# Queries and keys of stick-breaking heads as 2x2 block products behind the value projection, kept in DRAM

## The chip, the cores and the metric

One core of a Trainium2 chip runs the kernel. The metric is the device time in microseconds of one execution; the kernel before takes 1210.2 us (median of 3 runs, 1209.5 to 1210.64). TensorE (PE) multiplies matrices, VectorE (DVE), ScalarE (ACT) and GpSimd (POOL) work on elements, and SyncE (SP) issues nearly all transfers between DRAM and on-chip memory. Every engine works through its own queue in order; a wait at its head holds up all that stands behind it.

## The reference

One layer over 1024 frames of width 1024, in float32:

```python
h = rmsnorm(x, norm1_g)
proj = h @ w_in                      # 1024 x 3072
qa, ka, va, qb, kb, vb = split(proj) # 512 columns each: 8 heads of 64
ya = chunked_attention(qa, ka, va, rel_bias)      # group A: softmax over a band of 9 chunks
yb = stick_breaking_attention(qb, kb, vb)         # group B: causal, a cumulative product in place of softmax
x = x + concat(rmsnorm(ya, norm_a_g), rmsnorm(yb, norm_b_g)) @ w_out
x = x + conv_gated_mlp(rmsnorm(x, norm2_g), ...)  # up-projection, width-3 conv, silu gate, down-projection
return rmsnorm(x, final_g)
```

The change concerns the 1024 x 512 queries qb and the 1024 x 512 keys kb of group B.

## The kernel before, in words

Numbers are float32. Each operand of a large product is split into a high part (rounded to the format that TensorE takes) and a low part (the remainder), and a product is three matmuls: high x high, high x low, low x high (`mm3`, L144). `split` (L127) makes the two parts: a copy on ScalarE, then a subtraction, mostly on VectorE.

**Values first.** `all_v` (L241) makes the values of both groups as a product in 2 x 2 blocks with seven block products in place of eight (the Strassen-Winograd scheme). The normed input, without its row scale rn1, is h; split by features (k below or above 512) and frames (lo, hi), it gives the blocks b11, b21, b12, b22, of which b11, b21 and b22 are used as they are (tiles hh, hl), and four sums and differences t1 to t4, each of four tiles of 512 columns. The right-hand tiles of t1 and t3 share t_high[0] and t_low, one after the other; those of t2 and t4 share t_high[1]; t4's low parts lie where t3's were. Steps are pairs (p, k), product p and piece k, in the order p = 1, 2, 5, 6, 7, 3, 4. `extra(n)` (L385) hangs other work on a step: squares of x's rows for rn1, and at the last steps the results scaled by rn1 (`give`, L375), which go to DRAM (v_d). The four results c11 go first, then m5 and u2 (eight), and after the last step c21 (four).

**Pair 0 of group B.** Heads come in pairs n (0 to 3 are group B, 4 to 7 group A). Right behind v, L1105 to L1117 project query and key of pair 0 plainly: for each of two halves of the frames, 8 pieces of k with three matmuls, 48 matmuls for the query and 48 for the key; L1113 and L1115 in between spread rn1 over the columns (8 transposes). Each half is scaled, split and laid in the tiles qa, qb, ka, kb, la, lb that the scores want (`stack_q`, `stack_k`): a head's high and low rows on the two halves of the partitions.

**Attention with filler.** Group B (L1207 on) goes through 4 pairs x 8 query blocks x 2 heads = 64 items in the order ORDER_B; per item TensorE makes scores (zb), ScalarE a sigmoid, VectorE a scan (acts), and two items later TensorE transposes (tpb) and then multiplies with v (yb). Group A (L1266 on) goes through 4 pairs x 8 blocks with a softmax. Between these, TensorE gets filler: a generator (`filler`, L1126) gives the projections of pairs 1 to 7 in pieces of three matmuls, and then the group-B half of the output projection (pb). How much filler follows each item is set by RATE_B, LEAD_B, RATES_A and LEAD_A; `ready` (L1147) draws more when a planner (`Flow`, L485), which keeps a reckoned time for each engine, holds that the next step would wait. What filler is left after group A covers the norms there. For pairs 1 to 7 the second arrangement of the rows is made by on-chip transfers (`move`, L662).

The order on VectorE, ScalarE, GpSimd, SP and TensorE is that in which the code is written or the planner issues it; no scheduler reorders it. SP's transfers use eight semaphores in turn, so a transfer is issued only when the eighth one before it has landed.

Behind attention stand the rest of the output projection (pa), the up-projection (`up_pair`, L1772, which already uses seven products for the 2 x 2 blocks of each pair of column tiles), the convolution, and the down-projection, also in blocks.

Of the kernel before, what the change touches and what calls it, by code (L numbers as in the profile page):

```python
# [16 lines left out]
P = 128  # L17
T = 1024
# [18 lines left out]
RATE_B, LEAD_B = 19.0, 8.0  # L37
RATES_A, LEAD_A = (18.0, 22.0, 23.0, 20.0), 6.5
# [24 lines left out]
def tile_hybrid_block(  # L63
# [128 lines left out]
    with tc.tile_pool(name="kp", bufs=2) as kp:  # L192
# [42 lines left out]
        hh, hl, pre = [], [], []  # L235
# [5 lines left out]
        def all_v():  # L241
# [29 lines left out]
            ]  # L271
            row = area(kp.tile([P, D], F32, tag="rb", name="row", bufs=1))
# [47 lines left out]
            def factors(p, k):  # L320
# [14 lines left out]
                    4: (t_high[1][k], t_low[k], b[:, lo]),  # L335
# [3 lines left out]
            def parts(p, k):  # L339
                if p in (1, 2):  # L340
# [15 lines left out]
            raw0 = []  # L356
# [28 lines left out]
            def extra(n):  # L385
# [6 lines left out]
                if steps[n] == (7, 2):  # L392
                    for j in range(4):
                        S.copy(m5[j], X[j])
                    raw0.append(wp.tile([P, D], F32, tag="wr", name="raw0_0", bufs=1))
                    nc.sync.dma_start(raw0[0], w_in[12])
                if steps[n] == (3, 0):
                    for j in range(4):
                        plus(m5[j], m5[j], Y[j], V)
                if steps[n] == (3, 3):  # L400
# [3 lines left out]
                    raw0.append(kp.tile([P, D], F32, tag="rb", name="raw0_1", bufs=1))  # L404
                    nc.sync.dma_start(raw0[1], w_in[16])
# [6 lines left out]
                if steps[n] == (4, 2):  # L412
                    pre.append(weights(None, "qk01", raw=raw0[1]))
                if steps[n] == (4, 3):
                    give(staged("c21"), 1, 0, Y)

# [37 lines left out]
            for n, (p, k) in enumerate(steps):  # L454
# [16 lines left out]
                extra(n)  # L471

        S.preload_act_table_set("sqrt_and_others")
        all_v()
# [102 lines left out]

        class Banks:
# [19 lines left out]
        for n in range(1, 8):  # L598
            ct = 12 + n if n < 4 else n - 4
# [62 lines left out]
        def move(t, x, y, a, b):  # L662

            return load(128, lambda: nc.sync.dma_start(r32(x[b, t]), r32(y[a, t])))

        def stack_q(n, outs):
            s = 6 * (n % 2)
            qa, qb = slot(s, f"qa{n}", F32R), slot(s + 1, f"qb{n}", F32R)
            qk_of[n] = [qa, qb]

            def half(g):

                t, r = {}, rows(g)
                project = on_v(GW, lambda: scaled(outs[g], g, 0.125, f"q{n}", t))

                def low_rows(x, a, b):
                    return load(128, lambda: nc.sync.dma_start(r32(x[b, r]), t["f"][a, :]))

                if n == 0:
                    return fs.chain(  # L680
                        project,
                        on_s(GW, lambda: S.copy(qa[A, r], t["f"][A, :])),
                        on_s(GW, lambda: S.copy(qb[B, r], t["f"][B, :])),
                        on_v(GW, lambda: sub(qa[B, r], t["f"][A, :], qa[A, r]), "VL"),
                        on_v(GW, lambda: sub(qb[A, r], t["f"][B, :], qb[B, r]), "VL"),
                    )
                return fs.chain(
                    project,
                    on_s(GW, lambda: S.copy(qa[:, r], t["f"])),
                    on_v(GW, lambda: sub(t["f"].bitcast(F32R), t["f"], qa[:, r]), "VL"),  # L690
                    move(r, qb, qa, B, A),
                    low_rows(qb, B, B),
                    low_rows(qa, A, B),
                )

            for g in range(G):
                yield half(g)

        def stack_k(n, outs):
            s = 6 * (n % 2)  # L700
# [1480 lines left out]
```

## Time and profile before

| what | us |
| --- | --- |
| median of 3 runs | 1210.2 |
| profiled execution, span from first to last instruction | 1208.5 |
| TensorE busy | 1196.2 |
| VectorE busy | 922.2 |
| ScalarE busy | 676.1 |
| v in blocks ends, q of pair 0 begins | 85.98 |
| first scores of group B | 116.88 |
| up-projection in steady state | 606 to 980 |

In lists of instructions the columns are start, duration, engine, line, operation, output<-input, shapes and count; in a group's row the busy time, the mean in ns, then the idle time of the engine before it and what ended that. In rows of windows come the stretch, its length, the busy time of each engine with its count of instructions, the clock that TensorE was granted (1.00 is full), the busy share of the 16 DMA engines, and GB/s. TensorE's instructions overlap, so durations in a list add to more than the time passed; in the chain each has only its share.

### The profile page before, as it was taken

To read this page: it belongs to the slowest core of one execution; us is meant where nothing else is said; L and a number is where in the kernel's file an instruction comes from. 1 tells how busy PE (TensorE), PEld (TensorE's weight loads), DVE (VectorE), ACT (ScalarE), POOL (GpSimd) and SP (SyncE) were. 2 spreads that over 40 slices of the span, in tenths; PEclk is the share of its full clock that TensorE was granted. 3 is DMA by queue.
4 is the path that set the end of the run, shared out by engine and by line. 5 is a ranking of instruction groups with operands and counts; after the bars stand their busy time and mean duration, and the time that the engine had idled before them with its cause. 6 is when DMAs were issued, how large, how long until landed. Compare 5 with 4: busy or idle time off the path is not lost.

```text
span 1208.5 us, 17319 instructions
## 1 busy us (share of the span) xinstructions
PE 1196.2 (99%) x6476; PEld 997.9 (83%) x6476; DVE 922.2 (76%) x1405; ACT 676.1 (56%) x1196; POOL 178.9 (15%) x188
## 2 busy tenths in 40 slices
PE   9999999999999999999999999999999999999997
PEld 6788888888888888888878888888888888888887
DVE  7955776967676678568997877778677779969896
ACT  7864564656676657334665555555555455444424
POOL 0003211122213121232000000000000023132036
PEclk9999999999999999999999999999999999999998
DMA  8254343443534472143133222231222296420003
GB/s 300 92 186 141 85 134 79 133 113 100 162 84 101 128 227 82 37 147 114 36 105 105 71 87 88 70 105 70 87 88 71 71 374 252 182 97 1 1 1 140
DMA packets 64529, 137.30 MB, mean 114 GB/s; under 512 B 6839, under 2 KB 22327, under 8 KB 64446
## 3 DMA queue, kind: packets, MB, share of 16 engines
q1 hardware_dynamic: 64302, 136.10, 34.5%
q8 instruction: 51, 0.84, 0.3%
q14 instruction: 32, 0.26, 0.1%
q10 hardware_dynamic: 144, 0.11, 0.0%
HBM read 91.34 MB, written 28.33 MB: 99 GB/s over the span
## 4 chain that ended last, share of the span: by engine, by line
PE 93%; DVE 4%; ACT 2%; issue 1%; POOL 0%; DVEq 0%; ACTq 0%; POOLq 0%
PE u_c L1596 9%; PE u_e L1596 9%; PE u_a L1596 9%; PE dz L2095 8%; PE q_p L147 7%; PE k_p L147 7%; PE u_b L1596 5%; PE dj L2095 4%; PE dm L2095 4%; PE pb L147 3%; PE pa L147 3%; PE v_x L459 3%; PE tpb L874 3%; PE yb L888 3%; PE u L1648 3%; PE v_y L459 2%
## 5 line engine op out<-in xcount | busy, mean ns | idle before, releaser
L847 DVE TENSOR_TENSOR_SCAN acts<-zb,first 128x128 f32<-128x128 f32 (+7 forms) x64 | 86.6, 1353 | 39.6 <-ACT zb L856 39.3
L856 ACT ACTIVATE zb<-zb 128x128 f32<-128x128 f32 (+7 forms) x64 | 40.8, 637 | 55.0 <-PE zb L839 54.6
L125 POOL TENSOR_TENSOR dx_0wl<-dr,dx_0wh 128x512 fp32r<-128x512 f32 x1 | 1.4, 1366 | 412.6 <-ACT dx_0wh L1862 412.6
L1620 DVE SCALAR_TENSOR_TENSOR vt<-cv,cst,vt 128x1023 f32<-128x1023 f32 (+1 forms) x44 | 58.2, 1322 | 2.2 <-ACT vt L1614 1.4
L1620 DVE SCALAR_TENSOR_TENSOR gt<-cg,cst,gt 128x1023 f32<-128x1023 f32 (+1 forms) x44 | 56.4, 1281 | 1.4 <-ACT gt L1614 0.6
L969 ACT ACTIVATE pa<-sa,sta 128x640 f32<-128x640 f32 (+4 forms) x64 | 42.7, 668 | 23.1 <-DVE sta L955 21.2
L125 POOL TENSOR_TENSOR q_l<-q_r,q_h 128x256 fp32r<-128x256 f32 x28 | 22.2, 823 | 188.7 <-ACT q_h L629 188.7
L1614 ACT ACTIVATE gt<-cg,cst 128x1024 f32<-128x1024 f32 x22 | 27.4, 1246 | 37.0 <-DVE cg L1488 37.0
L147 PE MATMUL k_p<-hTh,k_h 128*128 128x512 f32 x112 | 47.7, 426 | 0.0
L147 PE MATMUL q_p<-hTh,q_h 128*128 128x512 f32 x112 | 46.5, 416 | 0.0
L878 ACT COPY tb<-tpb 128x128 f32<-128x128 f32 (+3 forms) x96 | 43.1, 485 | 5.8 <-PE tpb L874 4.7
L994 ACT COPY pta<-tpa 128x512 f32<-128x512 f32 (+3 forms) x80 | 36.1, 479 | 14.3 <-PE tpa L990 14.2
L147 PE MATMUL k_p<-hTh,k_l 128*128 128x512 f32 x112 | 43.9, 392 | 0.0
L147 PE MATMUL k_p<-hTl,k_h 128*128 128x512 f32 x112 | 43.9, 392 | 0.0
L147 PE MATMUL q_p<-hTh,q_l 128*128 128x512 f32 x112 | 43.8, 391 | 0.0
L147 PE MATMUL q_p<-hTl,q_h 128*128 128x512 f32 x112 | 43.8, 391 | 0.0
L955 DVE TENSOR_REDUCE sta<-sa 128x1 f32<-128x640 f32 (+4 forms) x64 | 42.0, 657 | 1.6
L874 PE MATMUL tpb<-ident,acts 128*128 128x128 f32 x288 | 42.9, 276 | 0.0
L1485 DVE TENSOR_TENSOR up_r<-up_r 128x512 f32<-128x512 f32 x60 | 41.3, 688 | 0.8
L990 PE MATMUL tpa<-ident,pa 128*128 128x128 f32 x240 | 39.0, 278 | 1.0 <-ACT pta L994 0.4
L874 PEld LDWEIGHTS tpb<-ident,acts 128*128 128x128 f32 x288 | 33.3, 141 | 5.4 <-issue 2.6
L990 PEld LDWEIGHTS tpa<-ident,pa 128*128 128x128 f32 x240 | 27.6, 140 | 9.5 <-issue 4.7
(1315 smaller groups left out, 3930.8 us busy)
## 6 DMA issues: line engine op xcount, KB each, us to landing
up_r<-in_w_up_dram SPq DMA_DIRECT2D x44, 512.0 KB, 3.5
act<-vt SPq DMA_DIRECT2D x22, 512.0 KB, 2.6
dr<-in_w_dn_dram SPq DMA_DIRECT2D x20, 512.0 KB, 6.3
dr<-act SPq DMA_DIRECT2D x20, 512.0 KB, 8.1
wv<-in_w_v_dram SPq DMA_DIRECT2D x16, 256.0 KB, 5.4
xin<-in_xT_dram SPq DMA_DIRECT2D x16, 256.0 KB, 5.4
row<-in_x_rows_dram SPq DMA_DIRECT2D x16, 256.0 KB, 2.6
v<-v_d SPq DMA_DIRECT2D x8, 512.0 KB, 5.9
```

What stands on the lines that cost most here:

```text
L147: PE.matmul(o, w[:, sl], t[:, rows(g)], start=first and i == 0, stop=last and i == 2,)
L459: PE.matmul(bank[j], t[:, cols(j)], w, start=p in (1, 5) and k == 0 and i == 0, stop=k == 3 and i == 2, skip_group_check=True,)
L847: V.tensor_tensor_scan(out=a[:, :w], data0=z, data1=first[:, :w], initial=1.0, op0=ALU.mult, op1=ALU.max,)
L874: PE.transpose(tp[:, cols(b)], self.a[h][:, cols(b0 + b)], ident)
L878: mine.append(flow.add(on_s(m * P, lambda o=o, tp=tp: S.copy(o, tp))))
L955: V.tensor_reduce(out=st[:, 0:1], in_=full, axis=AX.XY if nk == 5 else AX.X, op=ALU.max, negate=True,)
L969: on_s(w + 170, lambda: S.activation(po, full, AF.Exp, bias=st[:, 0:1], accum_out=st[:, 1:2])),
L990: PE.transpose(tp[:, cols(b)], self.pr[src][:, cols(c)], ident)
L1485: eng.tensor_tensor(out=out, in0=a, in1=b, op=ALU.subtract)
L1596: PE.matmul(o, w[:, cols(k)], t, start=start and k == 0 and i == 0, stop=k == 3 and i == 2, skip_group_check=True,)
L1620: V.scalar_tensor_tensor(out=t[:, : T - lag], in0=o[:, lag:], scalar=c1(c + ct), in1=t[:, : T - lag], op0=ALU.mult, op1=ALU.add,)
L2095: PE.matmul(o[m], w[:, cols(m)], t, start=i in (0, 1, 4, 5) and p == ps_[0] and j == 0, stop=p == ps_[-1] and j == 2, skip_group_check=True,)
```

## The change

Queries and keys of all four pairs of group B are made right behind v, by seven block products each pair; v's sums t1 to t4 are used again as right-hand blocks. The left-hand blocks come from the weights: q's two column halves (k below and above 512) are a11 and a12, k's second half a22, and s1 to s4 are sums of the halves.

- t1 and t2 are overwritten in v, so `keep` stores them to DRAM (16 transfers of 256 KB, in steps 9, 11, 12 and 14), and `bring_back` loads them again at step (4, 0) (8 transfers of 512 KB). t3 stays; t4 gets low tiles of its own (t4_low).
- `bring_raw` loads raw weights; `Pieces` makes sums and splits of a pair's weights. At steps (4, 0) to (4, 3) pair 0's first pieces are made.
- `early(n)` does a pair's seven products of 12 matmuls, in the order a11 b11, s1 t1, s2 t2, a12 b21, s3 t3, s4 b22, a22 t4 into three banks (eqk, eb, ec), and prepares pair n+1's pieces between them. The eight transposes for rn1 are in early(0). `early_out` scales, splits and stores each of the four results to DRAM.
- Pairs 4 to 7 are projected as before (96 matmuls each), but their results also go to DRAM (`spill_qk`); for every pair `load_qk` brings 12 transfers of 256 KB into the six tiles for the scores. `move`, `stack_q` and `stack_k` are gone.
- The filler is pairs 4 to 7 and the output projection, spread over both groups at lower rates; RATE_B and RATES_A are cut accordingly.

```diff
-RATE_B, LEAD_B = 19.0, 8.0
-RATES_A, LEAD_A = (18.0, 22.0, 23.0, 20.0), 6.5
+RATE_B, LEAD_B = 10.0, 4.0
+RATES_A, LEAD_A = (11.0, 13.0, 13.0, 13.0), 6.5
...
+            def bring_back():
+                for n in range(2):
+                    for k in range(4):
+                        t = slot(4 + k, f"t1_{k}", F32R) if n == 0 else kp.tile(
+                            [P, T], F32R, tag=f"y{k}", name=f"t2_{k}", bufs=1
+                        )
+                        nc.sync.dma_start(r32(t), t_d[n][k])
+                        again[n, k] = t[:, lo], t[:, hi]
...
                 if steps[n] == (4, 0):
-                    pre.append(weights(None, "qk00", raw=raw0[0]))
+                    bring_back()
+                    bring_raw(1, 11)
+                    ahead.append(Pieces(0))
+                    ahead[0].whole()
...
                 if steps[n] == (4, 3):
                     give(staged("c21"), 1, 0, Y)
+                    ahead[0].split("s2")
+                    bring_raw(1, 0)
+                    bring_raw(2, 1)
+                    bring_raw(2, 2)
+                    bring_raw(3, 3)
...
+        def product(o, left, what, start=True):
+            wh, wl = left
+            for k, (th, tl) in enumerate(right[what]):
+                for i, (w, t) in enumerate(((wh, th), (wh, tl), (wl, th))):
+                    PE.matmul(
+                        o, w[:, cols(k)], t, start=start and k == 0 and i == 0,
+                        stop=k == 3 and i == 2, skip_group_check=True,
+                    )
...
+            product(a, own.p["a11"], "b11")
+            S.copy(b, a)
+            if n == 0:
+                ob = big("rb1_ob")
+                across(ob[:, lo], rn1, 0, 4)
+                across(ob[:, hi], rn1, 4, 8)
+                S.copy(rb1, ob)
+                for what in ("s4", "s3"):
+                    own.make(what)
+                    own.split(what)
+            own.split("a22")
...
+            if nxt:
+                nxt.whole()
+                nxt.make("s1")
+                nxt.make("s2")
+            product(e, own.p["s1"], "t1")
+            S.copy(m5, e)
+            if nxt:
+                nxt.split("s1")
+            product(b, own.p["s2"], "t2", False)
+            S.copy(c, b)
+            S.copy(u2, b)
...
+            product(a, own.p["a12"], "b21", False)
+            early_out(n, "q", a, lo)
...
+            product(c, own.p["s3"], "t3", False)
+            plus(m5, m5, c, V)
+            early_out(n, "k", m5, hi, m5)
...
+            product(e, own.p["s4"], "b22", False)
+            plus(u2, u2, e, V)
+            early_out(n, "q", u2, hi, u2)
...
+            product(c, own.p["a22"], "t4", False)
+            early_out(n, "k", c, lo)
...
         def filler():
-            for n in range(1, 8):
+            for n in range(4, 8):
                 yield from project_qk(n)
+            while 4 not in rb_of:
+                yield None
```

How it stands on the queues, at two places. First SP, at the end of v. In before, from the last of the c11 results on (v_c is its fourth; xin0 to xin3 hold m5 and u2, v_d the values in DRAM, q1_r the raw query weights of pair 1):

```order
L381 DMA v_d0_111<-v_c_365 128x512
L383 DMA v_d0_111<-v_c_365 1x512
L381 DMA v_d1_112<-xin0_130 128x512
L381 DMA v_d1_112<-xin1_131 128x512
...
L381 DMA v_d1_112<-v_c_801 128x512
L613 DMA q1_r_816<-in_w_in_dram 128x1024
```

The same place now (t1_0 to t2_3 are the sums brought back, raw1_11 the raw query weights of pair 1 and raw1_0 its key weights):

```order
L399 DMA v_d0_111<-v_c_405 128x512
L401 DMA v_d0_111<-v_c_405 1x512
L372 DMA t1_0_792<-t_d0_0_129 128x1024
...
L372 DMA t2_3_806<-t_d1_3_136 128x1024
L529 DMA raw1_11_808<-in_w_in_dram 128x1024
L399 DMA v_d1_112<-xin0_170 128x512
...
L399 DMA v_d1_112<-v_c_878 128x512
L529 DMA raw1_0_890<-in_w_in_dram 128x1024
```

Nine loads of 512 KB have come between the first four results and the other twelve; the load of raw1_0 stands behind all of them, where that of q1_r stood.

Second ScalarE, behind the last result of v (v_c). In before the spread scale and the parts of pair 0 follow:

```order
L377 ACTIVATE v_c_801<-v_y3_96,rn1_77 128x512
L182 COPY rb1_810<-n1_0_rb_833 128x512
L182 COPY rb1_810<-n1_1_rb_845 128x512
L682 CAST qa0_851<-q0_f0_865 64x512
L683 CAST qb0_852<-q0_f0_865 64x512
```

Now (eb0, ec0 and eqk0 are round 0's banks; s1_1 is the sum s1 of pair 1, made by VectorE in place in raw1_0):

```order
L395 ACTIVATE v_c_878<-v_y3_96,rn1_77 128x512
L128 CAST s2_0_887<-raw0_q_665 128x512
L1213 COPY eb0_900<-eqk0_899 128x512
...
L128 CAST qk1wh_941<-raw1_11_808 128x1024
L1230 COPY em50_902<-eqk0_899 128x512
L128 CAST s1_1_960<-raw1_0_890 128x512
L1234 COPY ec0_901<-eb0_900 128x512
L1235 COPY eu20_903<-eb0_900 128x512
```

The copy into ec0, on which round 0's product s3 t3 is accumulated, stands behind the cast of pair 1's s1, which reads raw1_0.

More of the change, by code (lines that the diff above doesn't have):

```diff
@@ L1164, in need @@
                     done[0] += c
[L1165 to L1166 removed]
+                advance()
+            if n not in v_of:
+                raise RuntimeError("v was not asked for")
         meds, bigs = Banks(med, ready), Banks(big, ready)
```

290 lines of the change are left out of this document (179 added, 111 removed).

## The prediction

> **What bounds the kernel now.** I read the page first (engines' shares, the chain that ended last), then the windows by stage, then the timelines of the stretch that the change rebuilds.
>
> ```profile
> PE 1196.2 (99%) x6476; PEld 997.9 (83%) x6476; DVE 922.2 (76%) x1405; ACT 676.1 (56%) x1196; POOL 178.9 (15%) x188
> PE 93%; DVE 4%; ACT 2%; issue 1%; POOL 0%; DVEq 0%; ACTq 0%; POOLq 0%
> 85.98 4.10 PE q_p L147 x18
> 90.08 0.44 PE n_rb L177 x4
> 91.91 0.44 PE n_rb L177 x4
> 97.84 10.88 PE k_p L147 x48
> 617.75 2.72 PE u_c L1596 x12
> 125.00:500.00 375.00, 373.98 (x2787) 319.27 (x2786) 269.27 (x509) 228.97 (x477) 71.56 (x93) 1.00 0.41 116
> 606.00:980.00 374.00, 373.63 (x1647) 309.25 (x1648) 284.71 (x340) 207.86 (x302) 3.49 (x3) 1.00 0.27 93
> ```
>
> The second line is the chain that ended last: 93% of it is TensorE. The next five are pieces of that chain (start, length, count): 48 projection matmuls take 10.88 us and 12 of a product in blocks 2.72 us, 0.2267 us each in both forms. The last two are windows (busy of PE, PEld, DVE, ACT, POOL, then clock, DMA share, GB/s): through attention, 125 to 500 us, TensorE is idle for 1.0 us of 375; in the up-projection, whose scheme the change copies, for 0.4 of 374. So a matmul removed is time gained, as long as TensorE finds no new wait. The profiled execution has a span of 1208.5 us; the median of the runs is 1210.2, 1.7 more, and I add 1.7 to the sum. A difference under 0.2%, 2.4 us, I call the same, about what a measurement here can tell.
>
> **Part by part.**
>
> *Matmuls.* Query and key of a pair of heads took 2 x 2 x 8 x 3 = 96 matmuls, the seven products take 7 x 4 x 3 = 84; for four pairs 336 in place of 384. 48 x 0.2267 = 10.9 us leave TensorE. The eight transposes that spread rn1 stay. Some unknown is in the rate: in v, the product beginning at 52.44 ran slower than its neighbour.
>
> ```profile
> 52.44 11.45 PE v_y L459 x48
> 63.89 10.90 PE v_x L459 x48
> ```
>
> There the moving operand was a piece in tiles r0 to r3, where four left pieces of the new products now lie as stationary ones. The up-projection's pieces cost nothing so, and I take 0; with the whole difference it would be 336 x (0.2385 - 0.2271) = 3.8 us.
>
> *The vector work of a round.* One early round has 19 vector instructions of 512 columns and one of 1024.
>
> ```profile
> L1485 DVE TENSOR_TENSOR up_r<-up_r 128x512 f32<-128x512 f32 x60 | 41.3, 688 | 0.8
> L128 ACT CAST v_r<-wv 128x512 fp32r<-128x512 f32 x16 | 9.9, 618 | 2.1 <-DVE wv L225 1.1 <-PE v_y L459 0.7 <-DVE wv L228 0.3
> L1801 ACT COPY u_c<-u_b 128x512 f32<-128x512 f32 x19 | 11.0, 579 | 1.2 <-PE u_b L1596 1.2
> 87.47 1.23 DVE L125 TENSOR_TENSOR qk_l<-raw,qk_h 128x1024 fp32r<-128x1024 f32 x1 [4.64 <-ACT qk_h L128]
> ```
>
> That is 19 x 0.688 + 1.23 = 14.3 us beside 84 x 0.2267 = 19.0 us of TensorE: 75%, the same share at which the up-projection (284.7 of 374) leaves TensorE full. Rounds 1 to 3 I cost at their matmuls alone, but for 0.2 us (0 to 1) where round 1's first product waits for VectorE to read round 0's bank e.
>
> *The loads ahead of round 1's weights.* This decides the sum. SP's queue, windows of one microsecond (clock, DMA share, GB/s), and saturated stretches:
>
> ```profile
> 78.81 0.93 SPq L381 DMA_DIRECT2D v_d<-c  x2
> 82.22 3.14 SPq L381 DMA_DIRECT2D v_d<-xin  x5
> 89.92 0.41 SPq L381 DMA_DIRECT2D v_d<-v_c  x1
> 90.42 0.53 SPq L613 DMA_DIRECT2D q_r<-in_w_in_dram  x1
> 82.00:83.00 1.00, 1.00 0.65 231
> 83.00:84.00 1.00, 1.00 0.70 250
> 84.00:85.00 1.00, 1.00 0.67 254
> 85.00:86.00 1.00, 1.00 1.00 375
> 93.00:94.00 1.00, 1.00 1.00 393
> 94.00:95.00 1.00, 1.00 0.04 12
> 985.00:990.00 5.00, 5.00 (x24) 4.13 (x23) 4.96 (x5) 2.26 (x4) 2.25 (x2) 1.00 1.03 413
> raw<-in_w_in_dram SPq DMA_DIRECT2D x2, 512.0 KB, 3.5
> ```
>
> In before, v's results go out from 78.8 us; the load of q_r behind them is issued at 90.42 and the line of transfers runs empty at 94.0. In the changed order the eight loads of t1 and t2 and one raw weight, each of 512 KB, stand between the first four results (c11) and the other twelve, and raw1_0, the key half of round 1's weights, stands where q_r stood. Nine loads are 4.72 MB; at the 413 GB/s that 512 KB loads reached, 11.4 us. The line had 1.0 us of idle room from 82 to 85 (1 less 0.65, 0.70, 0.67). So raw1_0's last byte comes at 94.0 + 11.4 - 1.0 = 104.4, and I give 0.4 for its completion (a lone load takes 3.5 us for 1.3 us of bytes, so at most 2.2): 104.8.
>
> Who waits: VectorE's sum s1 of round 1 reads raw1_0; ScalarE's cast of that sum waits for it; and queued behind that cast on ScalarE is the copy of bank b into bank c of round 0, without which TensorE cannot begin t3. That is 0.69 + 0.62 + 0.58 = 1.9 us after landing: 106.7. TensorE starts round 0 at 85.98, where q_p stood, and has four products and the transposes to do before t3: 85.98 + 48 x 0.2267 + 2 x 0.44 = 97.7. It is idle for 9.0 us. From below: no completion and the line full throughout leave 8; from above: 375 GB/s (12.6 us), no room and 2.2 for completion make 13. t1 and t2 themselves arrive in time: t2's last, eighth of the nine, at about 83.5 + 8 x 0.524 / 0.413 = 93.7, wanted at 94.4.
>
> The Trainium skill, page DMA: Bandwidth & Descriptors, section Where 436 GB/s comes from, says that transfers between HBM and SBUF are bound at about 358 GB/s per core by the HBM. By that figure the nine loads take 13.2 us and the sum rises by 1.8. The row of 413 over five microseconds speaks against it here.
>
> *The clock after the wait.* TensorE's granted clock falls when it goes idle, and comes back late:
>
> ```profile
> 1200.00:1202.00 2.00, 1.18 (x8) 0.81 0.83 295
> 1202.00:1204.00 2.00, 0.00 (x0) 0.50 0.83 295
> 1.53 4.45 PE L214 MATMUL v_y<-zero 128*128 128x512 bf16 x10 [1.53 <-DVE zero L211]
> ```
>
> At the end of the kernel the clock is 0.81 and then 0.50 within some microseconds of the last dense work, and after the idle start ten 512-column matmuls take 4.45 us, 0.445 each. After nine idle microseconds I expect the same stretch at half speed: 10 x (0.445 - 0.227) = 2.2 us (from 0, if the clock holds, to 3).
>
> The Trainium skill, page TensorE: Matmul & The Clock Gate, section Part 1: The HAM clock gate, puts both the idle window that halves the clock and the busy one that restores it at about 3.4 us. By that the restart costs 3.4 x 0.5 = 1.7 us, and the sum is 0.5 less.
>
> *Attention.* Its filler is now pairs 4 to 7 and the output projection: 288 matmuls, 65.3 us, have moved ahead of it. TensorE's work there falls from 375 to 310 us; VectorE loses three pairs of 8 instructions, 16.5 us: 253 of 310, 82% in place of 72%. The stretch of the trace that comes nearest:
>
> ```profile
> 262.00:275.00 13.00, 13.00 (x127) 11.38 (x124) 12.70 (x16) 9.08 (x21) 2.87 (x4) 1.00 0.57 163
> PE tpa L990 <- ACT pta L994: 0.4, 2, 0.2
> ```
>
> In the fourth pass of group B, where the old order held only some three filler matmuls per item, VectorE was busy for 12.70 of 13 us and TensorE for 13.00. I take 0.5 us more idle in all (0 to 1.5; above that is a rival). The attention's queries and keys go through DRAM: per pair 2.1 MB out and 3.1 MB in, on engines at a 0.41 share, asked for a pass ahead; covered. If that cover went, a pair's 3.1 MB at 413 GB/s would show, 7.6 us.
>
> *The rest at nothing:* t4's own low parts (the same instructions into other tiles), and the sixteen 256 KB stores of t1 and t2 in v.
>
> ```profile
> 39.91 0.63 ACT L389 ACTIVATE row<-row 128x512 f32<-128x512 f32 x1 [0.94 <-DMA row<-in_x_rows_dram]
> 45.73 0.62 ACT L128 CAST th<-xin 128x512 fp32r<-128x512 f32 x1
> row<-in_x_rows_dram SPq DMA_DIRECT2D x16, 256.0 KB, 2.6
> ```
>
> The first stores follow this square of x's rows on SP's queue, at 40.6; four take 2.7 us of bytes and land by some 45, and the cast that writes their tile th again comes at 45.73. If that cover is gone, the cast waits for 1 us or so, and the rows of x behind them as much.
>
> *Sum:* 1208.5 - 10.9 + 9.0 + 2.2 + 0.2 + 0.5 = 1209.5, and 1.7 for the median: 1211.2 us, 1.0 above before. With the ends of the terms 1207.3 to 1221.6; most lies from 1208.5 to 1215.
>
> **Rivals.**
>
> *The wait is not there or is short (0.19).* If raw1_0 landed by 95.8, the copy into c would be in time, and no clock would be lost: 1210.2 - 10.9 + 0.7 = 1200.0; with half the wait about 1205. For it: my line of transfers is reckoned, not seen, and whether c waits hangs on one place in ScalarE's order. Against: the nine loads, the twelve stores of 256 KB and raw1_0 itself, 8.4 MB, from 82.2 to 95.8 would be 617 GB/s, where the fullest row has 413.
>
> *The line is slower than 413 (0.12).* If reads of freshly written DRAM, mixed with stores, run at the 375 of 85 to 86 us throughout, and each window of eight outstanding transfers leaves gaps, the wait is 12 and the sum 1214.2. For it: only stores and loads apart are seen at their best. By the Trainium skill's 358 GB/s, above, it would be 1213.0.
>
> *VectorE becomes the bound of attention (0.11).* Behind the last scores 72 matmuls of the output projection were left as cover; now 48. So 24 x 0.2267 = 5.4 us more filler has been drawn forward to fill waits that the order's planner foresaw. If the chip needs as much again, TensorE idles 5.4 us: 1216.6, slower. It decides from the point at which TensorE waits for VectorE's scans (acts) at more than a few transposes. Against it: the full 13 us above.
>
> **How the numbers follow.** My case has 0.58: of this 0.36 within 2.4 us, 0.17 slower, 0.05 faster. The short wait, 0.19, is faster; attention, 0.11, slower; the slow line slower at 0.10 and the same at 0.02. Faster 0.24, same 0.38, slower 0.38. The range takes in my case, the slow line, half of attention's case and the upper part of the short wait: 1203.5 to 1216.5.
>
> **What would show it.** Right: TensorE's longest wait of the whole profile in round 0, before the first t3 product, released by ScalarE's copy into c, with the cast of s1 and the landing of raw1_0 ahead of it; a granted clock under 1 behind it; rounds 1 to 3 at 19.0 us each; no wait over 0.5 us in attention. Wrong: round 0 ending near 106 with no gap, or gaps that recur in every round or at the scans.

## The result and the profile after

| | median of runs, us | lowest to highest | ratio to before, 95% interval |
|---|---|---|---|
| before | 1209.98 | 1209.50 to 1210.64 | |
| changed | 1243.36 | 1240.14 to 1245.49 | 1.0273 (1.0255 to 1.0291) |

The changed kernel is 33.4 us slower. Its profiled execution, the slowest of the four (1245.5 us), has a span of 1243.8 us, 35.3 more than that of before. The page's lines of busy time and of the chain that ended last:

```profile
PE 1199.5 (96%) x6428; PEld 992.8 (80%) x6428; DVE 944.2 (76%) x1443; ACT 688.3 (55%) x1225; POOL 153.2 (12%) x158
PE 66%; DVE 8%; DMA 6%; ACT 3%; issue 3%; POOL 1%; SPq 0%; DVEq 0%; ACTq 0%; POOLq 0%
```

TensorE has 48 instructions fewer, as the diff says, and yet 3.3 us more busy time; its idle time has gone from 12.3 us to 44.3. In the chain TensorE's share has fallen from 93% to 66%. The first product into the up-projection's bank b shows that hardly anything was lost behind attention: it starts at 606.37 us in before and at 640.90 now, 34.5 later.

The four early rounds run from 86.50 to 190.55 us. TensorE's timeline there (start, length, line, result and operands, count, and in brackets its idle time just before and what ended it), the rows with a wait:

```profile
91.02 3.13 PE L1180 MATMUL eqk<-t,s 128*128 128x512 f32 x12 [0.74 <-ACT eb L1213]
94.44 0.97 PE L1180 MATMUL eb<-t,s 128*128 128x512 f32 x3 [0.29 <-DMA t<-t_d]
95.70 0.97 PE L1180 MATMUL eb<-t,s 128*128 128x512 f32 x3 [0.29 <-DMA t<-t_d]
97.23 0.95 PE L1180 MATMUL eb<-t,s 128*128 128x512 f32 x3 [0.56 <-DMA t<-t_d]
98.84 0.97 PE L1180 MATMUL eb<-t,s 128*128 128x512 f32 x3 [0.66 <-DMA t<-t_d]
101.60 0.50 PE L1180 MATMUL eqk<-hTh,qk0wh 128*128 128x512 f32 x1 [1.79 <-ACT em L1230]
112.97 0.80 PE L1180 MATMUL ec<-th,s 128*128 128x512 f32 x1 [6.76 <-ACT ec L1234]
128.53 3.06 PE L1180 MATMUL eqk<-t,s 128*128 128x512 f32 x12 [1.44 <-ACT eb L1213]
149.92 3.06 PE L1180 MATMUL eqk<-t,s 128*128 128x512 f32 x12 [1.78 <-ACT eb L1213]
172.26 4.28 PE L1180 MATMUL eqk<-t,s 128*128 128x512 f32 x12 [2.73 <-ACT eb L1213]
```

Two kinds are to be seen. The rows for eb and ec are round 0 waiting for transfers. The rows for eqk recur in every round: eqk is the pair of banks a and e, and the product into e starts only when ScalarE has copied a into b (L1213), or the second product into a only when it has copied e into m5 (L1230). The ten waits sum to 17.0 us. The 336 matmuls and 8 transposes take 77.0 us at full clock, so of the 104.0 us another 10.0 went to matmuls at a lowered clock and to restarts behind waits. In the window 100 to 124 us the granted clock is 0.72:

```profile
100.00:124.00 24.00, 15.64 (x48) 12.11 (x49) 10.43 (x16) 5.52 (x9) 0.00 (x0) 0.72 0.70 246
```

Behind the rounds, group B starts with three more waits, and group A's attention has some where before had next to none. The rows of the timeline with a wait over 1 us, and the windows from 300 to 560 us of before and of the changed kernel, in this order (busy of PE, PEld, DVE, ACT, POOL, then clock, DMA share, GB/s):

```profile
200.08 0.35 PE L910 MATMUL zb<-la,qa 128*128 128x256 f32 x1 [3.13 <-DMA la<-kl_d]
219.97 0.35 PE L909 MATMUL zb<-kb,qb 128*128 128x256 f32 x1 [3.19 <-DVE acts L918]
383.90 0.85 PE L1061 MATMUL tpa<-ident,pa 128*128 128x128 f32 x6 [1.56 <-DVE sa L1022]
425.64 0.85 PE L1061 MATMUL tpa<-ident,pa 128*128 128x128 f32 x6 [1.56 <-DVE sa L1022]
540.21 1.06 PE L177 MATMUL na_rb<-ident,rn 128*128 128x128 f32 x8 [2.35 <-DVE rn L1105]
```

```profile
300.00:560.00 260.00, 258.67 (x1713) 218.50 (x1710) 181.94 (x406) 152.60 (x317) 65.65 (x76) 1.00 0.41 121
```

```profile
300.00:560.00 260.00, 252.04 (x1870) 212.29 (x1869) 189.10 (x411) 168.53 (x360) 54.13 (x69) 1.00 0.54 152
```

TensorE is idle for 8.0 us of these 260 instead of 1.3. The account of the profiled executions is then: 10.9 us of matmuls saved; 17.0 us of waits and 10.0 of clock and restarts in the rounds; 6.9 at the start of B (3.13, 0.60 and 3.19); 6.6 in attention. That gives 29.6 of the 35.3, counting the matmuls saved against the losses. Of the rest, 0.5 us lie ahead of the rounds, which begin at 86.50 where pair 0 began at 85.98, 0.8 lie behind attention, and about 1.5 are the clock at B's start (an estimate: 0.72 from 200 to 206 us, with TensorE busy for 5.32). Some 3 us stay without an account.

Why does c wait until 112.97? VectorE and ScalarE there, and SyncE's queue with the window of transfers around it:

```profile
108.36 0.69 DVE L125 TENSOR_TENSOR a22l<-raw,a22h 128x512 fp32r<-128x512 f32 x1 [13.19 <-DMA v_d<-v_c]
111.09 0.69 DVE L228 TENSOR_TENSOR raw<-raw 128x512 f32<-128x512 f32 x1 [0.90 <-DMA raw<-in_w_in_dram]
111.81 0.62 ACT L128 CAST s<-raw 128x512 fp32r<-128x512 f32 x1 [10.27 <-DVE raw L228]
112.34 0.58 ACT L1234 COPY ec<-eb 128x512 f32<-128x512 f32 x1
```

```profile
82.50 6.12 SPq L372 DMA_DIRECT2D t<-t_d  x8
90.66 5.38 SPq L399 DMA_DIRECT2D v_d<-xin  x5
103.34 1.29 SPq L399 DMA_DIRECT2D v_d<-c  x3
105.18 2.23 SPq L529 DMA_DIRECT2D raw<-in_w_in_dram  x4
```

```profile
82.00:90.00 8.00, 8.00 (x39) 6.55 (x39) 3.12 (x4) 8.00 (x15) 0.00 (x0) 1.00 0.87 282
90.00:100.00 10.00, 7.26 (x27) 4.06 (x25) 3.28 (x5) 3.60 (x6) 0.00 (x0) 1.00 1.02 384
```

The copy into c stands behind the cast of s1, which waits for round 1's key weights (raw, issued at 105.18, there at 111.09). VectorE would have been late in any case: the low part of a22 goes into the tile from which C21's last part is stored, and that store lands at 108.36. VectorE's two instructions behind it last until 110.19, so the weights add only 0.90 us to that: the two delays are nearly equal, and with one of them gone the other would have kept TensorE waiting almost as long. All of it stands in SyncE's queue behind the loads of t1 and t2.

### The profile page after: what moved, and what is told of

It is laid out like the page before. It is cut to its first block, busy times and chain, and to the rows that moved or that the text cites. A ratio compares the mean times of both kernels' runs of the same rounds, so it can differ in the third digit from the quotient of the medians.

```text
span 1243.8 us, 17412 instructions
## 1 busy us (share of the span) xinstructions
PE 1199.5 (96%) x6428; PEld 992.8 (80%) x6428; DVE 944.2 (76%) x1443; ACT 688.3 (55%) x1225; POOL 153.2 (12%) x158
## 4 chain that ended last, share of the span: by engine, by line
PE 66%; DVE 8%; DMA 6%; ACT 3%; issue 3%; POOL 1%; SPq 0%; DVEq 0%; ACTq 0%; POOLq 0%
PE u_a L1742 9%; PE u_c L1742 8%; PE u_e L1742 8%; PE dz L2241 8%; PE u_b L1742 4%; PE dj L2241 4%; PE dm L2241 4%; PE q_p L147 2%; PE tpb L945 2%; PE k_p L147 2%; PE yb L959 2%; PE pa L147 2%; PE dnl L2162 1%; DMA lb<-kl_d 1%; PE yy L1074 1%
## 5 line engine op out<-in xcount | busy, mean ns | idle before, releaser
L125 POOL TENSOR_TENSOR q_l<-q_r,q_h 128x256 fp32r<-128x256 f32 x16 | 13.3, 862 | 232.9 <-ACT q_h L740 208.9
L1929 ACT COPY u_b<-u_a 128x512 f32<-128x512 f32 x19 | 10.8, 571 | 38.1 <-PE u_a L1742 38.1
L1023 DVE TENSOR_TENSOR sa<-sa,bias 128x256 f32<-128x256 f32 (+1 forms) x64 | 26.2, 413 | 6.0 <-PE sa L1010 4.8
L1074 PE MATMUL yy<-pta,v 128*64 128x128 f32 x480 | 30.0, 276 | 0.0
L959 PE MATMUL yb<-tb,dv 128*64 128x128 f32 x448 | 29.5, 273 | 0.0
L125 POOL TENSOR_TENSOR wo_l<-wo_r,wo_h 128x256 fp32r<-128x256 f32 x28 | 20.1, 745 | 70.1 <-ACT wo_h L740 70.1
L1074 PEld LDWEIGHTS yy<-pta,v 128*64 128x64 f32 x480 | 26.1, 137 | 3.3 <-issue 1.1
```

The costliest lines, as they stand in the source:

```text
L959: PE.matmul(yy[HS[h], :], (d if j else v)[:, off : off + 64], self.at[h][:, self.c0[h] + j * P : self.c0[h] + (j + 1) * P], start=j == 0, ...
L1074: PE.matmul(yy[HS[h], :], v[:, (i + c) * P + h * 64 : (i + c) * P + (h + 1) * 64], self.pt[:, 4 * h + c if c < 4 else 8 + h, :], start=c = ...
```

## The experiments

All times are medians, with the ratio to runs of before beside them; the changed kernel stands at 1243.4 us, 1.0273 (1.0255 to 1.0291).

**e1_banks: the halves of one tile.**

```diff
-            z = big(f"eqk{n}")
-            a, e = z[:, lo], z[:, hi]
+            a, e = [big(f"{x}{n}")[:, :GW] for x in ("ea", "ee")]
...
-                ob = big("rb1_ob")
-                across(ob[:, lo], rn1, 0, 4)
-                across(ob[:, hi], rn1, 4, 8)
-                S.copy(rb1, ob)
+                for i, ob in enumerate((med("rb1_a"), pj("rb1_b"))):
+                    across(ob, rn1, 4 * i, 4 * i + 4)
+                    S.copy(rb1[:, halves[i]], ob)
```

> Edit: a and e of a round lie in two tiles of PSUM instead of the halves of one; the spread factors of round 0 go to two other banks. Theory (the changed kernel's first product e of a round waits for ScalarE's copy of a, because both are halves of one tile): the waits of 1.44, 1.78 and 2.73 us at the start of e in rounds 1, 2 and 3 go; those of 0.74 and 1.79 us in round 0 go too, but there the wait for c ends at 112.97 us whatever came before and takes them back. Sum -6.0 us and perhaps 1 us of clock behind the 2.73: about 1237 us. Rival (the waits come from ScalarE's place in its own queue or from the operand s1, and the copy only ends last by chance): another releaser takes their place, less than 1 us changes, 1242 to 1244.

1235.6 us, 1.0212 (1.0196 to 1.0227): -7.8. No wait for a copy of a or of e is left in any round. In round 0 the wait for c has grown by 3.8 us and ends 0.6 us earlier than it did:

```profile
112.41 0.80 PE L1180 MATMUL ec<-th,s 128*128 128x512 f32 x1 [10.59 <-ACT ec L1232]
```

So the waits at e were not for data or for a bank in use: the kernel's own ordering holds the two halves of a tile together, though they are two banks. With this edit the kernel does not compute the reference's result (it is off by 0.30, relative); why stays open. So e1 shows what the ordering costs and is no repair as it stands. e9, which computes the right result with a and e in two tiles in rounds 1 and 2 alone, has no wait before e in these rounds either.

**e2_no_reload: the loads of t1 and t2 left out.**

```diff
-                    bring_back()
...
-                "t1": [again[0, k] for k in range(4)],
-                "t2": [again[1, k] for k in range(4)],
+                "t1": list(zip(t_high[0], t_low)),
+                "t2": list(zip(t_high[1], t4_low)),
```

> Edit: the eight loads of t1 and t2 (4.2 MB) behind v are left out and the products with t1 and t2 read the tiles of t3 and t4, so the values of queries and keys differ; the stores stay. Theory (a line of transfers at 280 to 400 GB/s holds back both the store of C21, for which VectorE's low part of a22 waits until 108.4 us, and the load of round 1's key weights, which lands at about 111): without 4.2 MB in front both come about 10 us earlier, the waits of 1.8 us for t1 and t2 and of 6.8 us for c go, and the lowered clock behind them with some 4 to 5 us: about 1230 us. Rival (the order of ScalarE's and VectorE's instructions makes the wait, and the transfers only go with it): the wait for c keeps over 4 us, and the time stays above 1238.

1231.6 us, 1.0181 (1.0163 to 1.0200): -11.7. SyncE issues round 1's key weights 13 us earlier, VectorE passes a22 at 95.21 and s1 at 97.12, and no wait for c, t1 or t2 is left:

```profile
92.15 2.29 SPq L528 DMA_DIRECT2D raw<-in_w_in_dram  x4
...
95.21 0.69 DVE L125 TENSOR_TENSOR a22l<-raw,a22h 128x512 fp32r<-128x512 f32 x1 [0.26 <-DMA v_d<-v_c]
97.12 0.69 DVE L228 TENSOR_TENSOR raw<-raw 128x512 f32<-128x512 f32 x1
```

The rival falls: the same order of instructions does not wait for c when 4.2 MB are missing from the queue. The waits before e, 8.0 us in the four rounds, stay. Whether C21's store or the weights mattered more this run cannot tell, since both come earlier in it.

**e4_copies_first: the two copies ahead of the cast.**

```diff
-            if nxt:
-                nxt.split("s1")
             product(b, own.p["s2"], "t2", False)
             S.copy(c, b)
             S.copy(u2, b)
             if nxt:
+                nxt.split("s1")
                 nxt.split("s2")
```

> Edit: ScalarE's copies of b into c and u2 stand ahead of its cast of the next round's s1 in every round. Theory (VectorE is held as well: the low part of a22 waits for the store of C21 until 108.4 us and the sum s1 of round 1 for its weights until 111): the wait of 6.8 us for c goes, but the product with t4, which needs VectorE's sum into m5 behind these, now waits in its place; it began at 121.4 us and comes at 118 to 119: -2 to -4 us, about 1240. Rival (the place of the two copies in ScalarE's queue is the whole cause, as the prediction had it): 6.8 us and the clock behind it go, -9 to -11 us, 1233.

1242.9 us, 1.0274 (1.0259 to 1.0289): no difference that can be told. The wait for c is gone and a wait of 6.03 us stands one product later, where e waits for VectorE to read a (the halves again), and VectorE for the same store and the same weights:

```profile
115.58 0.80 PE L1180 MATMUL eqk<-hTh,s 128*128 128x512 f32 x1 [6.03 <-DVE eq0f L1190]
```

So the place in ScalarE's queue, which the prediction named, decides only which product meets the wait.

**e6_c21_queue: another queue for C21's store, another order in round 0.**

```diff
-                    nc.sync.dma_start(v_d[group][:P, o : o + GW], t)
+                    q.dma_start(v_d[group][:P, o : o + GW], t)
...
-                    give(staged("c21"), 1, 0, Y)
+                    give(staged("c21"), 1, 0, Y, nc.scalar)
```

and in early(0) the split of a22 and the whole of round 1's preparation behind the copies of b, its sums behind round 0's results.

> Edit: C21's four stores go through ScalarE's DMA queue instead of SyncE's, and in round 0 the low part of a22 and all preparation of round 1 stand behind the copies of b (the sums and splits of round 1 behind round 0's own results). Theory (round 0's wait for c is VectorE and ScalarE held behind C21's store, landing at 108.4 us, and round 1's key weights, at 111): the wait of 6.8 us and 3 us of lowered clock behind it go; a wait of 2 to 4 us for s1 comes at the start of round 1's product e, since its weights still land at about 110: -5 to -8 us, about 1237. Rival (only the weights' landing decides, whichever product meets it): the whole wait comes back in round 1: within 2 us of 1243.

1251.0 us, 1.0337 (1.0322 to 1.0353): +7.6, outside both. The first three of ScalarE's stores were issued 4 to 5 us apart, the copy of a into b behind them came at 103.82 instead of 90.38, and SyncE's five stores beside them took 9.63 us to issue instead of 5.38:

```profile
89.53 9.63 SPq L399 DMA_DIRECT2D v_d<-xin  x5
...
92.28 0.33 ACTq L399 DMA_DIRECT2D v_d<-c  x1
92.71 0.69 ACT L395 ACTIVATE c<-v_y,rn 128x512 f32<-128x512 f32 x1 [4.15 <-DMA t<-t_d]
96.24 0.33 ACTq L399 DMA_DIRECT2D v_d<-c  x1
...
103.82 0.58 ACT L1213 COPY eb<-eqk 128x512 f32<-128x512 f32 x1
```

The Trainium skill, page DMA: Bandwidth & Descriptors, section Issuing engines are not separate DMA queues, says that transfers run on the same 16 engines whoever issues them, and that issuing from several engines saves only the time of issuing. The trace fits the first part, by SyncE's stores that slowed down. Issuing itself was small here too, 0.33 us for each of ScalarE's stores; what kept ScalarE for some 13 us were the waits between them until other transfers had landed, as the row with 4.15 us shows. The new order of round 0 was not tried by itself, so what it is worth stays open.

**e7_clock: TensorE kept busy in the wait for c.**

```diff
+            if n == 0:
+                for i in range(28):
+                    PE.matmul(ob[:, lo], own.p["a11"][0][:, cols(0)], right["b11"][0][0], start=True, stop=True)
             product(c, own.p["s3"], "t3", False)
```

> Edit: 28 matmuls that nobody reads (6.3 us at 0.2267 us) stand ahead of round 0's first product with t3, in the time in which TensorE waits for c. Theory (the gaps of round 0 lower the granted clock, and the 14 or so matmuls behind the wait at 0.425 us instead of 0.2267 cost about 2.8 us): TensorE goes on at about 113 us as before, at full clock: -1.5 to -3 us, about 1241. Rival (the clock is lowered by something else than TensorE's own idle time, as the transfers): the granted clock behind the wait stays under 0.8 and the time within 1 us of 1243, or it rises by what the extra matmuls take beyond the wait.

1244.0 us, 1.0275 (1.0252 to 1.0298; four runs from 1239.4 to 1246.6). In the trace the clock did what the theory says, 1.00 from 100 to 124 us where the changed kernel had 0.72, with the transfers going on:

```profile
100.00:124.00 24.00, 20.10 (x86) 15.63 (x85) 13.61 (x20) 6.75 (x13) 0.00 (x0) 1.00 0.66 243
```

```profile
144.97 4.60 PE L1180 MATMUL eqk<-t,s 128*128 128x512 f32 x12 [1.79 <-ACT eb L1213]
```

The time did not follow: round 2 now ran twelve matmuls in 4.60 us where the changed kernel took 3.06, and the median is the same. The two traces do not settle it: e7's is of its fastest execution (1239.4 us) and the changed kernel's of its slowest, and in e7 C21's last store, ahead of which no transfer was moved, had landed at 105.43 instead of 108.36. That TensorE stays at full clock when it is kept busy through the wait is shown; what the clock costs the whole is not.

**e5_direct: the first pair's loads in one row.**

```diff
+            if n == 0:
+                for m in moves[0] + moves[1]:
+                    bring(*m)
+                qk_chains[0] = []
+                return
```

> Edit: the twelve loads of pair 0's queries and keys are issued by SyncE in one row behind the product with t2 of round 3, instead of being dealt out between round 3's stores by the planner. Theory (the loads are late because SyncE's queue holds them behind stores that wait for their data, the last at 195.94 us; the 64-row loads themselves take 3.1 MB at about 270 GB/s, 11.6 us, from 175.5 us on): all are there by 190 us, before the first scores at 196.7; the waits of 3.1 and 0.6 us and the lowered clock behind them (1.5 us) go, and part of the 3.2 us at the scans: -4 to -8 us, about 1237. Rival (the rate of the line at group B's start sets it, whoever is first): the stores of round 3 and the loads of v and of pair 1 are late in their place, and the scans wait longer: within 1.5 us of 1243.

1241.6 us, 1.0262 (1.0245 to 1.0279): -1.8, between the two and hardly to be told from none. The waits of 3.13 and 0.60 us for the pair's low keys are gone from the trace; the wait at the scans stays:

```profile
201.25 0.58 PE L914 MATMUL zb<-kb,qb 128*128 128x256 f32 x1 [2.69 <-DVE acts L923]
```

**e3_lead: more filler ahead of group B.**

```diff
-RATE_B, LEAD_B = 10.0, 4.0
+RATE_B, LEAD_B = 10.0, 14.0
```

> Edit: 14 us instead of 4 us of filler ahead of the first scores of group B, nothing else. Theory (the queries and keys of the first pair come through a line of transfers until 205 us, and nothing covers the last part): the waits of 3.1 and 0.6 us for the pair's low keys go, and the lowered clock behind them (about 2 us); the wait of 3.2 us at the scans behind a scaled half of q4, which waits for the second pair's loads, may stay or grow, since the filler itself is held by it: -3 to -8 us, 1236 to 1240. Rival (the filler is short already, and what is spent early is missed later in attention): the gain is given back by later waits, within 2 us of 1243.

1250.5 us, 1.0333 (1.0316 to 1.0351): +7.1, beyond the rival. The waits for the low keys are gone, those at the scans have grown to 2.0 and 3.9 us, and what was spent early is missing at the end: 10.5 us idle from 300 to 560 us instead of 8.0, and the last factors of group A wait 5.22 us instead of 2.35:

```profile
300.00:560.00 260.00, 249.49 (x1896) 210.58 (x1893) 194.58 (x414) 172.02 (x370) 49.48 (x62) 0.99 0.53 152
```

```profile
546.12 1.94 PE L177 MATMUL na_rb<-ident,rn 128*128 128x128 f32 x8 [5.22 <-DVE rn L1105]
```

**e8_three_rounds: pair 3 given back to the filler.**

```diff
-RATE_B, LEAD_B = 10.0, 4.0
-RATES_A, LEAD_A = (11.0, 13.0, 13.0, 13.0), 6.5
+RATE_B, LEAD_B = 14.5, 4.0
+RATES_A, LEAD_A = (14.0, 16.0, 16.0, 17.0), 6.5
...
-        for n in range(4):
+        for n in range(3):
             early(n)
...
-            for n in range(4, 8):
+            for n in range(3, 8):
                 yield from project_qk(n)
```

> Edit: only pairs 0 to 2 are made behind v; pair 3 is a projection of 96 matmuls (21.8 us) among the filler as the pairs of group A, through the same stores and loads, and the rates of filler are raised to 14.5 in group B and 14, 16, 16, 17 in group A. TensorE has 12 matmuls more (2.7 us). Theory (filler too thin for attention costs 6.8 us: 1.6 and 1.6 us at the transposes, 2.3 at the last factors of group A, 1.0 and smaller; a fifth pair gives a quarter more filler): round 3's own waits go (2.7 us and 1.3 of clock), attention's waits fall by half (3 us), 2.7 us of matmuls come: -2 to -6 us, about 1239. Rival (attention's waits come from stores and loads of pairs through the DMA queues): they stay or grow with one more pair going that way, and the time is 1242 to 1247.

1232.4 us, 1.0187 (1.0171 to 1.0202): -11.0, more than either. TensorE's idle time from 300 to 560 us is 1.9 us, nearly that of before, with one pair more going through DRAM by the late way, which refutes the rival:

```profile
300.00:560.00 260.00, 258.06 (x1872) 219.71 (x1871) 183.90 (x409) 166.76 (x352) 55.56 (x70) 1.00 0.55 156
```

The wait of 3.19 us at the scans in B's start has gone with it; the wait for the low keys is still there, 4.11 us. The edit does two things at once, more filler and no round 3, whose wait before e of 2.73 us goes with the round.

**e9 to e12: the repairs together.** e9 is e8 with e5's loads and with a and e apart in rounds 1 and 2. e10 makes pair 0 by the eight products and the other three by seven, in e11 only pairs 1 and 2 are made by seven, pair 3 being filler. e12 is e11 with another order of transfers. The code that e10 adds:

```diff
+        def plain():
+            own = ahead[0]
...
+            for j in range(4):
+                what, g = "qk"[j // 2], j % 2
+                for k in range(KT):
+                    mm3(outs[j : j + 1], *own.p[what], cols(k), hh[k], hl[k], k == 0, k == KT - 1, (g,))
```

> Edit: three early pairs with pair 3 as filler (as in e8), with a and e of rounds 1 and 2 in two tiles (as in e1) and pair 0's loads in one row (as in e5). Theory (separate causes add up): from e8's 1232.4 us the waits of 1.4 and 2.7 us before e in rounds 1 and 2 and the 4.1 us for the pair's low keys with some clock go: 1223 to 1226. Rival (they hide one another: what is gained in the rounds is waited for at the loads): 1229 or more.

e9: 1230.8 us, 1.0176 (1.0159 to 1.0193): as the rival has it. The waits before e in rounds 1 and 2 and for the low keys are gone, but TensorE now waits 3.29 us at the end of the rounds for VectorE to empty bank c, and 2.65 at the scans. Round 0 is as it was; its wait for c is 4.97 us.

> Edit: pair 0 is made by the eight products as 96 plain matmuls from hT, and only pairs 1 to 3 by seven, so that t1, t2, C21's store and round 1's weights have 21.8 us of matmuls that need none of them; with a and e in two tiles and pair 0's loads in one row. Theory (round 0 waits for the line of transfers behind v, and its waits lower the clock): 11.1 us of waits in round 0 and about 4 us of clock go for 2.7 us of matmuls; 0.5 to 3 us come for s1 at round 1; the waits before e (5.9 us) and about 2 us at B's start go; attention's 6.8 us stay: 1222 to 1227. Rival (the wait is not for the transfers but for the chain of small VectorE and ScalarE instructions that prepares a round): it moves to round 1 with over 5 us, 1230 or more.

e10: 1238.0 us, 1.0230 (1.0214 to 1.0245): as the rival's number has it; round 0 has no wait, and round 1 has one of 9.26 us:

```profile
121.41 4.88 PE L1185 MATMUL ee<-t,s 128*128 128x512 f32 x12 [9.26 <-ACT s L128]
115.99 0.62 ACT L1200 CAST eq0h<-eq0f 128x512 fp32r<-128x512 f32 x1 [8.74 <-DMA qh_d<-eq0h]
```

The second row tells why: on ScalarE, ahead of the cast of s1, stands the high half of pair 0's second result, and it waits 8.74 us for the store of the first to free one of the three buffers; the store was issued at 108.19 behind five 512 KB loads of weights. The place is the rival's, the cause in the trace is the line.

> Edit: as e10, and pair 3 is a projection among the filler as in e8, so only pairs 1 and 2 are made by seven products. Theory (thin filler is a cause of its own): 2.7 us of matmuls come on top of e10 and 5 us of attention's waits go, as round 3's do: 2 to 6 us less than e10; counted from before, 24 matmuls fewer (-5.4 us) and 3 to 10 us of waits and clock left: 1209 to 1217. Rival (what helped in e8 was only that round 3 with its waits fell away, and e10's edits have removed these already): within 2 us of e10.

e11: 1230.3 us, 1.0166 (1.0151 to 1.0182): 7.7 less than e10. In the traces TensorE's idle time from 300 to 560 us has fallen from 6.8 us to 2.7, so thin filler counts by itself; but another 3.1 us come from round 1's waits, 9.0 us in place of 12.1, at which the edit did not aim. It is not near the account from before, for round 1 still waits 6.80 and 2.22 us.

e12 differs from e11 in the order of the loads:

```diff
-                    bring_back()
                     bring_raw(1, 11)
...
                     bring_raw(1, 0)
-                    bring_raw(2, 1)
-                    bring_raw(2, 2)
+                    bring_back()
```

> Edit: on top of e11, the eight loads of t1 and t2 stand behind round 1's weights instead of ahead of v's last stores, and the two loads for pair 2's weights stand behind pair 0's last stores; no instruction of VectorE, ScalarE or TensorE is moved. Theory (the line of transfers behind v alone holds VectorE and ScalarE, through the three buffers of the halves on their way to DRAM, and so round 1): the waits of 6.8 and 2.2 us in round 1 fall under 2 us together and 2 to 3 us of lowered clock with them: 1218 to 1222. Rival (the chain of small VectorE and ScalarE instructions for pair 0's four results and for s1 is too long by itself): over 4 us of round 1's waits stay, 1225 or more.

e12: 1226.8 us, 1.0141 (1.0123 to 1.0160): -3.4 to e11, and 5.5 us of round 1's waits stay, the rival's numbers. The first wait fell from 6.80 to 2.67 us with nothing moved but transfers; the second did not:

```profile
115.40 4.87 PE L1182 MATMUL ee<-t,s 128*128 128x512 f32 x12 [2.67 <-ACT s L128]
123.11 4.61 PE L1182 MATMUL eb<-t,s 128*128 128x512 f32 x12 [2.84 <-ACT eb L1253]
109.99 0.62 ACT L1197 CAST eq0h<-eq0f 128x512 fp32r<-128x512 f32 x1 [7.44 <-DMA qh_d<-eq0h]
```

The second, 2.84 us, is the copy of a into b standing on ScalarE behind two casts of the round's preparation, the first of which waited 2.09 us for VectorE. So both theories have a part: the line made most of the first wait, ScalarE's order the second. The third row shows that e12 does not free ScalarE of the line: the cast of pair 0's second result still waits 7.44 us for the store of the first, which now stands behind the loads of t1 and t2. What is left of the first wait may therefore be the line's too. No version here beats before: e12, the best, saves 24 matmuls, 5.4 us, and is still 17 us behind.

## Why the prediction was wrong

It forecast 1211.2 us, range 1203.5 to 1216.5. By its steps:

*Matmuls, -10.9 us:* right. 48 instructions are gone, and rows at full clock stand 0.227 us apart as before.

*The wait for c, 9.0 us, and the clock behind it, 2.2:* the links that the prediction named are all there (longest wait of the profile, released by ScalarE's copy into c, behind the cast of s1, behind round 1's key weights), and the size was too small. Round 0 takes 37.7 us (86.50 to 124.20) against 19.9 of work: 17.8 us lost, not 11.2. The wait for c itself is 6.76 us, less than forecast, but only because TensorE came to it late; t3 begins at 112.97 us instead of 106.7. The step that failed is the rate of the line. It was put at 413 GB/s, taken from five microseconds of weight loads; loads of freshly stored tiles mixed with stores ran at 282 GB/s from 82 to 90 us and 384 from 90 to 100, 321 over the whole way from 82.2 to 111.1, and the weights came at 111.1 instead of 104.8. By the Trainium skill's 358 GB/s (page DMA: Bandwidth & Descriptors, section Where 436 GB/s comes from), which the prediction set aside, the estimate is 106.6: nearer, and still too early, since the line did not hold that rate either. "t1 and t2 themselves arrive in time" failed with the rate (1.8 us), and two waits for the halves of one tile, 0.74 and 1.79, took another 2.5. The wait of VectorE for C21's store, 13.19 us, was not seen in the order at all. It hides behind the weights, which end VectorE's idle time only 0.90 us later: with the weights in time t3 would have begun hardly earlier. The clock's cost was put too low as well: behind the wait for c 24 matmuls took 8.46 us (112.97 to 121.43) instead of 5.44, which is the upper end of the stated 0 to 3, and the waits of under 2 us ahead of it, for which nothing was reckoned, were followed by matmuls at half clock too (101.60 to 105.2 us).

*Rounds 1 to 3 at their matmuls alone, +0.2 us:* this step failed outright. Three times 84 x 0.2267 are 57.1 us; the timeline has 66.3 (124.20 to 190.55), 9.2 more. The argument was one of load, 75% of VectorE beside TensorE, as in the up-projection. It said nothing of the instruction that each product waits for. In each round the product into e stands behind a copy out of a, because both are halves of one tile; e1 takes this away and gains 7.8 us. Of the round's four banks the prediction looked at e in one place only, across rounds.

*Attention, +0.5 us, with loads "covered":* wrong twice. At B's start the loads of pair 0 are not asked for a pass ahead, as they are for later pairs; they come behind round 3's stores, at 267 GB/s with the DMA engines full. The rows are a store and the load behind it in the chain, a wait of VectorE ahead of the scans, and the window:

```profile
190.91 5.01 DMA qh_d<-eq3h
195.94 9.06 DMA lb<-kl_d
215.52 1.77 DVE L876 TENSOR_TENSOR dv<-v,dv 128x1024 f32<-128x1024 f32 x1 [3.04 <-DMA v<-v_d]
```

```profile
196.00:208.00 12.00, 8.27 (x33) 6.10 (x32) 5.36 (x7) 3.06 (x6) 0.00 (x0) 0.86 1.11 267
```

That is 6.9 us of waits, near the 7.6 that the prediction gave for a cover that is gone: 3.7 for the pair's low keys, and 3.19 at a scan that comes late because VectorE waited 3.04 us for a load of v in the same line. What they cost is less sure: in e5 the 3.7 us were gone and the kernel was 1.8 us faster. And the filler was too thin for attention: 6.6 us more idle time, which was the rival of 5.4 us (chance 0.11), though at the transposes and the last factors rather than at the scans; e3 and e8 move it in both directions.

Together the missed parts are 6.6 in round 0, 9.0 in rounds 1 to 3, 6.9 at B's start and 6.1 in attention: 28.6 of the 34.3 us by which the profiled span, 1243.8, exceeds the 1209.5 that the prediction's sum gave for it. The row named as proof against, "gaps that recur in every round or at the scans", is what the profile shows.

## What to carry to other kernels

Before costing a product at its matmuls, write down for each bank which instruction must have read it, and ask whether the ordering sees banks or whole tiles: here two banks in one tile were one thing to wait for. When a step through DRAM is added, count what stands behind it in the issuing queue, stores that free a buffer above all, and take the rate of such a mix, not the best of plain loads. Filler moved out of a stage takes its cover along: of the 10.9 us of matmuls saved here, 6.6 were lost again in attention, where the filler had hidden the waits.

## What the runs showed of the hardware that was not expected

A full line of transfers does not keep one pace from execution to execution: C21's last store had landed at 108.4 us in the changed kernel, at 105.6 in e5 and 105.4 in e7, whose edits move no transfer ahead of it. The times spread too: four runs of before lie within 1.1 us, of the changed kernel within 5.4, of e7 within 7.2. That the line makes this spread is not shown; e1's runs, with the same line, lie within 1.7.

At group B's start, where loads into 64 rows, loads of v and stores run together, 268 GB/s moved from 188 to 220 us with all DMA engines busy, against 384 from 90 to 100 us, where all but some one-row transfers have 128 rows. The row count was not changed alone, and from 82 to 90 us transfers of 128 rows moved no more than 282, at a DMA share of 0.87.

The clock behind a wait of the same length was not always the same. Twelve matmuls took 3.06 us behind 1.78 us of waiting in round 2 of the changed kernel and 4.28 behind 2.73 in its round 3; in e7 they took 4.60 behind 1.79, and in e8 3.06 behind 2.73:

```profile
151.64 3.06 PE L1179 MATMUL eqk<-t,s 128*128 128x512 f32 x12 [2.73 <-ACT eb L1212]
```

The Trainium skill, page TensorE: Matmul & The Clock Gate, section Part 1: The HAM clock gate, has a window of about 3.4 us that runs freely and halves the clock after an idle one. That it runs freely fits these rows; that a wait of 1.79 us was enough in one of them does not fit an idle window of 3.4.
